# Key and rate products made beside attention instead of in the scan's prep

## The chip, the cores and the metric

The kernel runs on one core of a Trainium2 chip. The core has a matrix engine (TensorE, in the profile PE, its weight loads PEld), a vector engine (VectorE, DVE), an activation engine (ScalarE, ACT), a general engine (GpSimd, POOL) and a queue engine for transfers (SyncE, SP). All work from one on-chip memory; transfers to and from the DRAM run on 16 DMA engines. The metric is the device time of one execution in microseconds (us).

## The reference, cut to what matters

One layer of an encoder: a feed-forward block, a mixing block, a second feed-forward block, for 1024 tokens of width 1024. The mixing block has two groups of 8 heads of 64: attention with three dilated windows, and a recurrent group (RWKV-7) with a forward and a backward scan. What the change touches is the input of the scan:

```python
w_logit = w0 + jnp.einsum('bsdr,drc->bsdc', jnp.tanh(wd), w2)
decay = jnp.exp(-jnp.exp(-jax.nn.softplus(-w_logit) - 0.5))
a = jax.nn.sigmoid(a0 + jnp.einsum('bsdr,drc->bsdc', ad, a2))
kk = (k * k_k).reshape(B, S, H, N)
kk = kk / jnp.maximum(jnp.sqrt(jnp.sum(kk * kk, axis=-1, keepdims=True)), 1e-12)
k_dir = k[:, :, None, :] * (1.0 + (a - 1.0) * k_a)
...
xs = (orient(both(r)), orient(decay), orient(k_dir), orient(both(v)),
      orient(both(kk)), orient(kk[:, :, None, :] * a))
...
    sa = jnp.einsum('dbhvk,dbhk->dbhv', state, kk)
    state = state * w[..., None, :] - sa[..., :, None] * kka[..., None, :] + v[..., :, None] * k[..., None, :]
```

So the scan takes, for each of two directions (`d`), two products that depend on the rate `a`: `kk * a` (here the **rate product**) and `k * (1 + (a - 1) * k_a)` (the **key product**). The second is also used after the scan, for the bonus term.

## The kernel before, in words

The kernel is one program for one core, about 41,000 instructions, all in fp32. `run` (L1167) goes through these stages: first feed-forward; low-rank rates (`low_rank`, L534) and attention's projections; attention; the scan; the finish of the recurrent group; the output projection; the second feed-forward.

**The order of the work.** The program is written against a tile layer: tiles come from pools, a tag in a pool has a number of buffers (`bufs`), and a tile that reuses a buffer waits until all readers and writers of the old tile are done. When the program is built, a planner fixes the order of each engine's queue from the order in the text, priorities and its own estimates of durations; so instructions of neighbouring parts are interleaved. On the chip each queue, SP's and POOL's among them, runs strictly in that order: an instruction that waits holds up all that stand behind it on its engine.

**Streams.** `project_rwkv` (L499) makes one 128-column stream of the recurrent group for all 1024 tokens: it loads columns of `w_in` (tiles `zraw`, halves `zh` and `zl`), multiplies (L510, matmuls `zr`), mixes in the neighbouring tokens (`shift`, L517, its two VectorE steps L524 and L525) and hands the stream, tile `us`, to `stream` (L566). Streams 0 to 3 are r, 4 to 7 are k, 8 to 11 are v. For a k stream, `stream` stores k (L579), normalises it per head (L583 to L599, tile `kr`) and stores that (L600), both by POOL's queue, into the DRAM tensor `rk_d`, in which r, k and kk lie behind one another.

**Attention** (`attention`, L737) goes through 8 heads. In each, `near` (L665) makes scores (L684, L685), subtracts the maximum (VectorE L686), exponentiates (ScalarE L689), transposes (L698, copies L699) and multiplies by the values (L705); the head ends with steps on VectorE (L719 to L729), POOL (L731 to L733) and VectorE (L734). Behind head h one stream is written, in the order 4, 5, 6, 7, 1, 2, 3; in the trace its matmuls lie between those of the heads. Attention's tiles come from the pool `wa` (2 buffers a tag), those of the streams from `zr` (2 buffers a tag where nothing else is said).

**The scan** works in 8 blocks of 128 tokens, each in both directions.
- `prep(n)` (L789) makes for each direction the factors of block n. It loads the summed decays (`th_w`), the rates (`th_a`) and r, k and kk together (`in`, 768 KB in one transfer, one buffer), all for 4 x 128 channels and 128 tokens. Then: exponentials (L811, L812), products with kk and r (L816, L817), the rate product (L820: `(th_a + 1) * kk`, L821: times 0.5 and the inverse decay), the key product (ScalarE L825, four instructions, one for each 128 channels, then VectorE L827), its product with the inverse decay (L828), and a store of the key product (L829, SP's queue, to `kd_d`). Matmuls L836 and VectorE L838 make the small triangular matrices `lm`, transposes L844 and ScalarE L846 the tile `bt`. Part of `lm` goes out to the DRAM (L852).
- `solve(n)` (L856) loads it back in another layout (tile `X`) and inverts on VectorE in 62 small dependent steps (L872, L874) and a transpose (L876).
- `merge(n)` (L879) finishes the inverses with small matmuls (L889, L894, L900).
- `chain(n)` (L918) takes the state through the two 64-token chunks of the block: matmuls L941, L952, L937, copies on ScalarE (L944, L954, L970), the new state on VectorE (L968).

Three sets of block tiles exist, and prep n+3 is written behind chain n (L1300 to L1305). Preps 0 and 1 are written among the four value streams (L1272 to L1275).

**The finish** (`finish_unit`, L975) adds both directions and loads for that, among others, the two key products (`k0`, `k1`, L983).

Of the kernel before, what the change touches and what calls it, by code (L numbers as in the profile page):

```python
# [10 lines left out]
F32 = mybir.dt.float32  # L11
F32R = mybir.dt.float32r
AF = mybir.ActivationFunctionType
OP = mybir.AluOpType
# [4 lines left out]
S, D, DFF, INW = 1024, 1024, 2816, 3456  # L19
# [7 lines left out]
C, NC_, BLK = 64, 16, 2  # L27
TB = C * BLK
# [135 lines left out]
class _Kernel:  # L164
# [333 lines left out]

    def project_rwkv(self, p, psum, x, blocks):  # L499

        nc, V, A, T = self.nc, self.nc.vector, self.nc.scalar, self.nc.tensor
        for c0, n in blocks:
            hl = self.columns(p, ATT + c0 * 128, n * 128)
            for ct in range(c0, c0 + n):
                cs = slice((ct - c0) * 128, (ct - c0 + 1) * 128)
                ps = [psum.tile([128, 512], F32, name="zr", tag="d", bufs=2) for half in range(2)]
                for half in range(2):
                    for k, (h, l) in enumerate(hl):
                        for i, (w, j) in enumerate(((h, 0), (h, 1), (l, 0))):
                            T.matmul(ps[half], w[:, cs], x[half][j][:, k, :], start=(k == 0 and i == 0),  # L510
                                     stop=(k == NK - 1 and i == 2))
# [54 lines left out]
    def stream(self, p, psum, ct, y):  # L566
# [10 lines left out]
        elif ct < 8:  # L577
            i = ct - 4
            self.nc.gpsimd.dma_start(self.rk_d[4 + i], y)  # L579
            sq = p.tile([128, S], F32, name="ksq", tag="u", bufs=1)  # L580
            kr = p.tile([128, S], F32, name="kr", tag="kr", bufs=1)
# [11 lines left out]
            for half in range(2):  # L593
# [195 lines left out]
    def prep(self, n, p, psum, big):  # L789
# [8 lines left out]
        for d in range(2):  # L798
            b = n if d == 0 else NC_ // BLK - 1 - n
            ts = slice(b * TB, (b + 1) * TB)  # L800
            th = {}
            for nm in "wa":
                th[nm] = p.tile([128, 4, TB], F32, name="th_" + nm, tag="th_" + nm, bufs=2)
                self.load(th[nm], self.lr_d[nm][d][:, :, ls].rearrange("a p t -> p a t"))
            x3 = p.tile([128, 3, 4, TB], F32, name="in3", tag="in3", bufs=1)
            self.load(x3.rearrange("p j a t -> p (j a) t"), self.rk_d[:, :, ts].rearrange("a p t -> p a t"))
            x = {nm: x3[:, j, :, ::-1] if d else x3[:, j] for j, nm in enumerate(("r", "k", "kk"))}
            cum = th["w"]
            e1 = self.e1
# [9 lines left out]
            bb = bk[:, :, :, 0:C]  # L819
            V.scalar_tensor_tensor(bb, chunks(th["a"]), 1.0, chunks(x["kk"]), op0=OP.add, op1=OP.mult)  # L820
            V.scalar_tensor_tensor(bb, bb, 0.5, ei, op0=OP.mult, op1=OP.mult)  # L821
            A.copy(bk[64:, :, :, 2 * C:], bk[64:, :, :, 0:C])
            kd = th["a"]
            for pr in range(4):
                A.activation(kd[:, pr, :], kd[:, pr, :], AF.Identity, scale=self.kah[:, pr:pr + 1],  # L825
                             bias=self.ka1[:, pr:pr + 1])
            V.tensor_tensor(kd, kd, x["k"], op=OP.mult)  # L827
            V.tensor_tensor(bk[:, :, :, C:2 * C], chunks(kd), ei, op=OP.mult)  # L828
            self.nc.sync.dma_start(self.kd_d[d][:, :, ls].rearrange("a p t -> p a t"), kd)  # L829
            bt = big.tile([128, BLK, 2, 4, 64], F32, name="bt", tag=f"bt{d}")  # L830
# [144 lines left out]
    def finish_unit(self, p, psum, b, g, x, g2w):  # L975
# [6 lines left out]
        z = {}  # L982
        for nm, src, sl in (("y0", self.y_d[0], ts), ("y1", self.y_d[1], back), ("k0", self.kd_d[0], ts),  # L983
                            ("k1", self.kd_d[1], back), ("r", self.rk_d, ts), ("v", self.v_d, ts)):
            z[nm] = p.tile([128, 2, FB], F32, name="f_" + nm, tag="f_" + nm)
            self.load(z[nm], src[ps2, :, sl].rearrange("a p t -> p a t"))
# [112 lines left out]
    def constants(self):  # L1099
# [67 lines left out]
    def run(self):  # L1167
# [5 lines left out]
        with self.top as top:  # L1173
# [87 lines left out]
            zr, pz = self.pool(s_zr, "zr", 2), self.pool(s_zr, "ps_r", 1, space=PSUM)  # L1261
            streams = [4, 5, 6, 7, 1, 2, 3]
            self.attention(pa, wa, lambda h: self.project_rwkv(zr, pz, x, [(ct, 1) for ct in streams[h:h + 1]]))
            s_at.close()
# [175 lines left out]
```

## Time and profile before

| | |
|---|---|
| median of 3 runs | 2351.09 us (2346.66 to 2355.77) |
| the profiled execution | 2345.14 us |
| its span, first to last instruction | 2343.4 us |
| busy share: PE, DVE, ACT, POOL | 94%, 75%, 44%, 24% |
| attention | about 905 to 1190 us of the span |
| first preps with value streams | about 1190 to 1290 us |
| scan | about 1290 to 1565 us |
| finish | about 1565 to 1640 us |

How to read it: times in the views are microseconds from the start of the span. A row of a group names line, engine, operation, the tile written <- the tiles read, shapes and count, then the busy time of the group in us and the mean of one in ns, then the idle time of the engine ahead of it and what ended it. A row of waits names who waited, for whom, the total in us, how many times, and the longest. A row of the timeline has start, duration, engine, line, operation, tiles, shapes and count, and in brackets the idle time ahead and its end. Durations of neighbouring instructions on one engine overlap a little, so what one costs its queue is the distance between starts. A matmul's busy time is modelled; a busy PE isn't PE at its peak.

### The profile page before, as it was taken

Reading aid. Unit: us, or ns where it says so; the run is one execution under the profiler, and the core shown is the slowest. Engines: PE = TensorE matmul, PEld = TensorE weight load, DVE = VectorE, ACT = ScalarE, POOL = GpSimd, SP = SyncE. Lnnn points to the kernel's source line nnn. Section 1 sums busy time; section 2 is a strip of 40 time slices with the busy share of each in tenths; the row PEclk is TensorE's granted clock in tenths of the full one; section 3 lists DMA queues with packets and bytes.
Section 4 is the critical chain, followed back from the end, with each engine's and each line's share of the span. In section 5 each row is a group of like instructions: output and inputs, shape, how many; then the busy total and the mean of one; then the engine's idle time right before and its main releaser. Section 6 shows DMA issues by size and latency. Waiting matters only on the chain. (4 is left out here: it accounts for less than half of the span.)

```text
span 2343.4 us, 41364 instructions
## 1 busy us (share of the span) xinstructions
PE 2204.7 (94%) x15556; PEld 1783.2 (76%) x15556; DVE 1766.4 (75%) x2870; ACT 1032.5 (44%) x1958; POOL 552.9 (24%) x662
## 2 busy tenths in 40 slices
PE   6999999999999998999996889988799999999997
PEld 4788888878877676788775777765578888887886
DVE  8899999965676244666668878737899999996565
ACT  4333232354567412666545565445442323235453
POOL 6244444410000010111111111122334444441000
PEclk8999999999999999999997899999899999999999
DMA  5344545476661514443268656368434454548555
GB/s 158 99 165 159 173 147 171 161 265 194 196 223 80 219 46 118 119 118 97 64 171 219 170 150 172 106 200 278 153 117 166 167 175 147 173 155 267 192 191 179
DMA packets 357149, 381.97 MB, mean 163 GB/s; under 512 B 73043, under 2 KB 264403, under 8 KB 356949
## 3 DMA queue, kind: packets, MB, share of 16 engines
q1 hardware_dynamic: 309088, 278.53, 39.1%
q0 software_dynamic: 27504, 88.14, 10.0%
q10 hardware_dynamic: 20356, 12.66, 1.8%
q8 instruction: 122, 2.00, 0.4%
q14 instruction: 79, 0.64, 0.1%
HBM read 256.49 MB, written 122.75 MB: 162 GB/s over the span
## 5 line engine op out<-in xcount | busy, mean ns | idle before, releaser
L186 ACT ACTIVATE wh<-raw 128x512 fp32r<-128x512 f32 (+1 forms) x273 | 167.5, 626 | 261.2 <-DVE raw L62 92.2
L187 DVE TENSOR_TENSOR wl<-raw,wh 128x512 fp32r<-128x512 f32 (+1 forms) x273 | 277.3, 1018 | 3.2 <-ACT wh L186 2.3
L81 PE MATMUL gu<-xh,wh 128*128 128x512 f32 x704 | 277.7, 395 | 1.2 <-ACT xh L186 0.8
L81 PE MATMUL gu<-xl,wh 128*128 128x512 f32 x704 | 276.3, 392 | 0.0
L81 PE MATMUL gu<-xh,wl 128*128 128x512 f32 x704 | 275.9, 392 | 0.0
L415 PE MATMUL pd<-gl,gwh 128*128 128x512 f32 x616 | 240.4, 390 | 2.6 <-DVE gl L187 2.6
L415 PE MATMUL pd<-gh,gwh 128*128 128x512 f32 x616 | 239.5, 390 | 0.6 <-DVE row L86 0.6
L415 PE MATMUL pd<-gh,gwl 128*128 128x512 f32 x616 | 239.7, 389 | 0.0
L86 DVE TENSOR_TENSOR row<-gu,row 128x512 f32<-128x512 f32 x308 | 206.7, 683 | 22.1 <-PE gu L81 21.5
L187 DVE TENSOR_TENSOR gwl<-graw,gwh 128x512 fp32r<-128x512 f32 (+1 forms) x176 | 118.0, 674 | 128.6 <-ACT gwh L186 126.5
L116 POOL DMA_DIRECT2D d_hid<-row x154 | 85.1, 553 | 471.8 <-DVE row L114 446.1
L186 ACT ACTIVATE gwh<-graw 128x512 fp32r<-128x512 f32 (+1 forms) x176 | 101.3, 576 | 186.7 <-PE pd L415 152.2
L81 PEld LDWEIGHTS gu<-xh,wh 128*128 128x128 f32 x704 | 133.7, 190 | 30.3 <-ACT xh L186 2.0
L81 PEld LDWEIGHTS gu<-xh,wl 128*128 128x128 f32 x704 | 133.4, 190 | 27.7
L81 PEld LDWEIGHTS gu<-xl,wh 128*128 128x128 f32 x704 | 133.4, 190 | 27.4
L415 PEld LDWEIGHTS pd<-gl,gwh 128*128 128x128 f32 x616 | 115.7, 188 | 28.1 <-DVE gl L187 4.4
L415 PEld LDWEIGHTS pd<-gh,gwh 128*128 128x128 f32 x616 | 115.6, 188 | 25.3 <-DVE row L86 1.0
L415 PEld LDWEIGHTS pd<-gh,gwl 128*128 128x128 f32 x616 | 115.7, 188 | 23.9
L94 ACT ACTIVATE row<-row 128x512 f32<-128x512 f32 x44 | 27.9, 633 | 227.1 <-DVE row L86 219.6
L187 DVE TENSOR_TENSOR gl<-raw,gh 128x512 fp32r<-128x512 f32 x160 | 112.2, 713 | 15.6 <-ACT gh L186 15.1
L145 POOL TENSOR_TENSOR ws<-ws 128x512 f32<-128x512 f32 x88 | 114.4, 1300 | 1.2
L186 ACT ACTIVATE gh<-raw 128x512 fp32r<-128x512 f32 x160 | 98.1, 621 | 36.4 <-DMA raw<-in_ffn_w_down_dram 21.7
(354 smaller groups left out, 5258.8 us busy)
## 6 DMA issues: line engine op xcount, KB each, us to landing
d_hid<-row POOLq DMA_DIRECT2D x154, 256.0 KB, 2.4
graw<-d_hid SPq DMA_DIRECT2D x132, 256.0 KB, 2.9
raw<-in_ffn_w_gate_dram SPq DMA_DIRECT2D x88, 256.0 KB, 3.1
raw<-in_ffn_w_up_dram SPq DMA_DIRECT2D x88, 256.0 KB, 3.3
ws<-in_ffn_w_down_dram SPq DMA_DIRECT2D x88, 256.0 KB, 4.4
d_ws<-ws POOLq DMA_DIRECT2D x88, 256.0 KB, 2.3
raw<-d_ws SPq DMA_DIRECT2D x88, 256.0 KB, 2.7
raw<-in_ffn_w_down_dram SPq DMA_DIRECT2D x66, 256.0 KB, 3.5
```

The source lines that it names most:

```text
L81: self.K.nc.tensor.matmul(ps, a[:, k, :], b[:, k, :], start=(k == 0 and i == 0), stop=(k == 3 and i == 2))
L86: add = lambda o, x: V.tensor_tensor(o, ps, x, op=OP.add)
L94: A.activation(y[:, 0], y[:, 0], AF.Silu)
L116: put = lambda n, y: G.dma_start(self.hid[n - 1, j // 2], y)
L145: G.tensor_tensor(o, a, b, op=OP.subtract)
L186: self.nc.scalar.activation(h, src, AF.Copy)
L187: (eng or self.nc.vector).tensor_tensor(l, src, h, op=OP.subtract)
L415: T.matmul(ps[x], a[:, ts], b, start=(m == 0 and k == 0), stop=(m == NM - 1 and k == 2))
```

## The change

Both products are made once, for all 1024 tokens, when a key stream is made beside attention. For each key stream and direction a tile `ra` of 128x1024 rates is loaded by SP's queue from `lr_d` (512 KB), ahead of the stream's columns, into a tag of its own in attention's pool (two buffers, so 8 KB more of each partition). In `stream`, behind the normalised key, ScalarE and VectorE make the key product in two halves of 512 tokens (tiles `rb`, in the tag `vts`, two buffers, which only the value streams used), VectorE makes the rate product in one instruction of 1024 tokens in place, and POOL's queue stores them: two stores of 256 KB and one of 512 KB. The backward direction reads k and kk in reverse. The plain k is no longer stored.

`prep` loads four things instead of three: decays, the rate product (`ka`, two buffers), the key product (`kd`, one buffer), and r and kk (`in2`, 512 KB, one buffer). The instructions L820, L825 and L827 and the store L829 go; the one that was L821 now reads `ka` and L828 reads `kd`. The finish reads the key products from the new tensors `ak_d`.

```diff
-    def project_rwkv(self, p, psum, x, blocks):
+    def project_rwkv(self, p, psum, x, blocks, wide=None):
         for c0, n in blocks:
+            for d in range(2) if 4 <= c0 < 8 else ():
+                a = wide.tile([128, S], F32, name="ra", tag="ra")
+                self.load(a, self.lr_d["a"][d][c0 - 4])
+                self.rates.append(a)
             hl = self.columns(p, ATT + c0 * 128, n * 128)
...
         elif ct < 8:
             i = ct - 4
-            self.nc.gpsimd.dma_start(self.rk_d[4 + i], y)
...
-            self.nc.gpsimd.dma_start(self.rk_d[8 + i], kr)
+            self.nc.gpsimd.dma_start(self.rk_d[4 + i], kr)
+            for d in range(2):
+                a = self.rates.pop(0)
+                turned = lambda z: z[:, ::-1] if d else z
+                for half in range(2):
+                    sl = slice(half * 512, half * 512 + 512)
+                    b = p.tile([128, 512], F32, name="rb", tag="vts")
+                    A.activation(b, a[:, sl], AF.Identity, scale=self.kah[:, i:i + 1], bias=self.ka1[:, i:i + 1])
+                    V.tensor_tensor(b, b, turned(y)[:, sl], op=OP.mult)
+                    self.nc.gpsimd.dma_start(self.ak_d[d][4 + i][:, sl], b)
+                V.scalar_tensor_tensor(a, a, 1.0, turned(kr), op0=OP.add, op1=OP.mult)
+                self.nc.gpsimd.dma_start(self.ak_d[d][i], a)
...
-            th = {}
-            for nm in "wa":
-                th[nm] = p.tile([128, 4, TB], F32, name="th_" + nm, tag="th_" + nm, bufs=2)
-                self.load(th[nm], self.lr_d[nm][d][:, :, ls].rearrange("a p t -> p a t"))
-            x3 = p.tile([128, 3, 4, TB], F32, name="in3", tag="in3", bufs=1)
+            cum = p.tile([128, 4, TB], F32, name="th_w", tag="th_w", bufs=2)
+            self.load(cum, self.lr_d["w"][d][:, :, ls].rearrange("a p t -> p a t"))
+            ak = [p.tile([128, 4, TB], F32, name=nm, tag=nm, bufs=b) for nm, b in (("ka", 2), ("kd", 1))]
+            for j in range(2):
+                self.load(ak[j], self.ak_d[d][4 * j:4 * j + 4, :, ls].rearrange("a p t -> p a t"))
+            x3 = p.tile([128, 2, 4, TB], F32, name="in2", tag="in2", bufs=1)
             self.load(x3.rearrange("p j a t -> p (j a) t"), self.rk_d[:, :, ts].rearrange("a p t -> p a t"))
...
-            V.scalar_tensor_tensor(bb, chunks(th["a"]), 1.0, chunks(x["kk"]), op0=OP.add, op1=OP.mult)
-            V.scalar_tensor_tensor(bb, bb, 0.5, ei, op0=OP.mult, op1=OP.mult)
+            V.scalar_tensor_tensor(bb, chunks(ak[0]), 0.5, ei, op0=OP.mult, op1=OP.mult)
             A.copy(bk[64:, :, :, 2 * C:], bk[64:, :, :, 0:C])
-            kd = th["a"]
-            for pr in range(4):
-                A.activation(kd[:, pr, :], kd[:, pr, :], AF.Identity, scale=self.kah[:, pr:pr + 1],
-                             bias=self.ka1[:, pr:pr + 1])
-            V.tensor_tensor(kd, kd, x["k"], op=OP.mult)
-            V.tensor_tensor(bk[:, :, :, C:2 * C], chunks(kd), ei, op=OP.mult)
-            self.nc.sync.dma_start(self.kd_d[d][:, :, ls].rearrange("a p t -> p a t"), kd)
+            V.tensor_tensor(bk[:, :, :, C:2 * C], chunks(ak[1]), ei, op=OP.mult)
...
-        self.rk_d, self.v_d = self.dram("rk", [12, 128, S]), self.dram("v", [4, 128, S])
+        self.rk_d, self.v_d = self.dram("rk", [8, 128, S]), self.dram("v", [4, 128, S])
...
-        self.kd_d = [self.dram(f"kd{d}", [4, 128, S]) for d in range(2)]
+        self.ak_d = [self.dram(f"ak{d}", [8, 128, S]) for d in range(2)]
```

More of the change, by code (lines that the diff above doesn't have):

```diff
@@ L982, in finish_unit @@
         z = {}
-        for nm, src, sl in (("y0", self.y_d[0], ts), ("y1", self.y_d[1], back), ("k0", self.kd_d[0], ts),
-                            ("k1", self.kd_d[1], back), ("r", self.rk_d, ts), ("v", self.v_d, ts)):
+        for nm, src, sl in (("y0", self.y_d[0], ts), ("y1", self.y_d[1], back), ("k0", self.ak_d[0][4:], ts),
+                            ("k1", self.ak_d[1][4:], back), ("r", self.rk_d, ts), ("v", self.v_d, ts)):
             z[nm] = p.tile([128, 2, FB], F32, name="f_" + nm, tag="f_" + nm)
@@ L1261, in run @@
             zr, pz = self.pool(s_zr, "zr", 2), self.pool(s_zr, "ps_r", 1, space=PSUM)
-            streams = [4, 5, 6, 7, 1, 2, 3]
-            self.attention(pa, wa, lambda h: self.project_rwkv(zr, pz, x, [(ct, 1) for ct in streams[h:h + 1]]))
+            streams, self.rates = [4, 5, 6, 7, 1, 2, 3], []
+            self.attention(pa, wa, lambda h: self.project_rwkv(zr, pz, x, [(ct, 1) for ct in streams[h:h + 1]], wa))
             s_at.close()
```

3 lines of the change are left out of this document (1 added, 2 removed).

## The prediction

> **What bounds the kernel now.** I read the views in this order: the page's head, the busy time of each engine in windows cut at the stage borders, the engines' waits inside the two stages that the change touches, and VectorE in order of time.
>
> ```profile
> span 2343.4 us, 41364 instructions
> PE 2204.7 (94%) x15556; PEld 1783.2 (76%) x15556; DVE 1766.4 (75%) x2870; ACT 1032.5 (44%) x1958; POOL 552.9 (24%) x662
> ```
>
> By the page TensorE bounds everything. The windows below split that average; their columns are the span of the window, the busy time (and instructions) of PE, PEld, DVE, ACT and POOL, then the granted clock, the DMA share and GB/s. The first is attention, the second the first preps with the value streams, the third the scan up to the last full solve.
>
> ```profile
> 905.00:1190.00 285.00, 276.34 (x2665) 222.98 (x2664) 168.79 (x453) 163.96 (x384) 37.58 (x55) 0.98 0.39 107
> 1190.00:1290.00 100.00, 77.48 (x768) 63.07 (x768) 79.86 (x204) 56.80 (x110) 11.17 (x19) 0.83 0.80 211
> 1290.00:1500.00 210.00, 188.20 (x3621) 157.43 (x3622) 165.71 (x480) 113.24 (x214) 28.27 (x53) 0.91 0.57 155
> ```
>
> In attention PE is busy 276.3 of 285 us: it sets the pace, and VectorE (169) and ScalarE (164) have over 110 us to spare each. From 1190 to 1500 PE leaves 310 - 265.7 = 44.3 us idle, and its clock is 0.83 and 0.91. VectorE in order of time shows what it waits for: the end of one block's solve (L876) and the first product of the next (L872).
>
> ```profile
> 1257.47 1.05 DVE L876 STREAM_TRANSPOSE X<-Ti 128x512 f32<-128x512 f32 x1
> 1258.44 0.15 DVE L872 TENSOR_TENSOR ttmp<-X,Ti 128x31 f32<-128x31 f32 x1
> ...
> 1339.65 1.06 DVE L876 STREAM_TRANSPOSE X<-Ti 128x512 f32<-128x512 f32 x1
> 1341.27 0.19 DVE L872 TENSOR_TENSOR ttmp<-X,Ti 128x31 f32<-128x31 f32 x1 [0.56 <-DMA X<-d_x]
> ...
> 1498.18 1.06 DVE L876 STREAM_TRANSPOSE X<-Ti 128x512 f32<-128x512 f32 x1
> 1501.32 0.19 DVE L872 TENSOR_TENSOR ttmp<-X,Ti 128x31 f32<-128x31 f32 x1 [0.86 <-DMA X<-d_x]
> ```
>
> One solve follows another with a gap of 1 to 3 us, and merge and chain of a block can only start behind its solve. Seven solves end from 1257.5 to 1498.2, six steps of 40 us. In those 40 us VectorE's one queue also holds the prep of a later block, two directions of it. So from 1190 to 1500 VectorE's queue, its work plus its waits, is the path. The waits in 1190 to 1500:
>
> ```profile
> DVE ttmp L872 <- DMA X<-d_x: 10.4, 4, 5.8
> DVE sv L968 <- PE st L937: 9.3, 6, 3.8
> DVE lm L838 <- PE lp L836: 9.0, 11, 2.0
> DVE pr L816 <- DMA in<-d_rk: 6.6, 5, 2.0
> DVE th_a L827 <- ACT th_a L825: 6.5, 5, 2.0
> ```
>
> **What the scan loses (removed).** One direction of a prep, on VectorE:
>
> ```profile
> 1214.17 0.68 DVE L816 TENSOR_TENSOR pr<-in,e 128x512 f32<-128x512 f32 x1
> 1214.77 0.69 DVE L817 TENSOR_TENSOR pr<-in,e 128x512 f32<-128x512 f32 x1
> 1215.38 0.68 DVE L820 SCALAR_TENSOR_TENSOR bk<-th_a,in 128x512 f32<-128x512 f32 x1
> 1215.98 0.28 DVE L187 TENSOR_TENSOR zl<-zraw,zh 128x128 fp32r<-128x128 f32 x1
> 1216.18 0.68 DVE L821 SCALAR_TENSOR_TENSOR bk<-bk,th_w 128x512 f32<-128x512 f32 x1
> 1218.56 0.69 DVE L827 TENSOR_TENSOR th_a<-th_a,in 128x512 f32<-128x512 f32 x1 [1.69 <-ACT th_a L825]
> 1219.28 0.69 DVE L828 TENSOR_TENSOR bk<-th_a,th_w 128x512 f32<-128x512 f32 x1
> ```
>
> L820 and L827 go; L821 and L828 stay with other operands. Each is shown with 0.68 us, but starts are 0.60 us apart (1214.17, 1214.77, 1215.38), so one costs its queue 0.60. There are 16 of each:
>
> ```profile
> L820 DVE SCALAR_TENSOR_TENSOR bk<-th_a,in 128x512 f32<-128x512 f32 x16 | 11.0, 688 | 1.6 <-DMA in<-d_rk 1.4
> L827 DVE TENSOR_TENSOR th_a<-th_a,in 128x512 f32<-128x512 f32 x16 | 11.0, 688 | 6.6 <-ACT th_a L825 6.5
> L825 ACT ACTIVATE th_a<-th_a,ka,kah 128x128 f32<-128x128 f32 x64 | 28.3, 486 | 5.3 <-DVE bk L820 5.1
> ```
>
> 32 x 0.60 = 19.2 us leave VectorE, all inside 1190 to 1500. Not all reaches the end: PE is itself 86% busy there, and where VectorE comes earlier it meets a later PE or DMA (the 10.4, 9.3 and 9.0 above). The bounds are 0 and -19.2; I take two thirds, -13, because the waits listed are the minority of VectorE's 310 us.
>
> The 64 ACTIVATEs of L825 (28.3 us) leave ScalarE, which is busy 170 of 310 us; by themselves nothing. But they stand between L820 and L827, and VectorE waits 6.5 us for them. Also, the tile "in" has one buffer, and L827 is its last reader, 4.4 us behind L816; afterwards L817, 0.6 us behind, is the last reader, so that part of the 6.6 us waits for the next load goes. Bounds 0 and -13.1. What is late next is the tile "kd", one buffer too: its load waits for the L828 of the direction before, on SP's queue, with the load of r and kk written behind it; both wait for less than the old load did, as L828 now follows without ScalarE. I take half of the 6.5, -3.
>
> **Transfers and queues of the scan.** Median landing times, KB each:
>
> ```profile
> in<-d_rk SPq DMA_DIRECT2D x16, 768.0 KB, 5.9
> th_a<-d_a SPq DMA_DIRECT2D x16, 256.0 KB, 5.7
> d_kd<-th_a SPq DMA_DIRECT2D x16, 256.0 KB, 2.8
> ```
>
> Per direction SP issued three loads and a store, and will issue four loads: no change in SP's issue time. Bytes fall from 256+256+768+256 = 1536 to 1280 KB. A third of "in" becomes the tile kd; a 256 KB load lands after 5.7 us and a 768 KB one after 5.9, so the loads are no faster. The store waited for L827 with later loads behind it; that block goes. I count 0, inside the bounds above. The final stage reads the key product from the new tensors, written long before: nothing on the path, 0.
>
> **What attention gains (added).** Four key streams, two directions each: 8 STTs of 128x1024 and 16 products of 128x512 on VectorE, 16 ACTIVATEs of 128x512 on ScalarE, 24 new stores and 4 dropped on POOL's queue, 8 loads on SP's. The nearest rows in 905 to 1640:
>
> ```profile
> L524 DVE SCALAR_TENSOR_TENSOR us<-u,c_rwkv_mu_prev,us 128x1023 f32<-128x1023 f32 x12 | 15.4, 1280 | 11.9 <-ACT us L523 11.8
> L523 ACT ACTIVATE us<-zr,mu 128x512 f32<-128x512 f32 x22 | 15.1, 686 | 0.8 <-POOL ya L732 0.8
> L579 POOL DMA_DIRECT2D d_rk<-us x4 | 2.3, 584 | 21.2 <-ACT sb L631 5.3 <-DVE us L525 5.3 <-issue 5.3
> ```
>
> VectorE: 8 x 1.28 + 16 x 0.60 = 19.8 us. ScalarE: 16 x 0.69 = 11.0. POOL: 20 x 0.58 = 11.7, on an engine that is busy 37.6 of 285. The work does not shrink, it moves: VectorE gets back what it gave, at a place where it is not the pace. VectorE goes from 59 to 66% busy there, ScalarE from 58 to 61%. The cover is PE's 276 us. If all of it were gone the cost would be 19.8 for VectorE or more by a wait (below). PE's own waits in attention say how thin the cover is:
>
> ```profile
> PE zr L510 <- ACT zh L186: 2.6, 1, 2.6
> PE pt L637 <- ACT sb L631: 2.3, 1, 2.3
> PE s L626 <- DMA qp<-d_q: 1.7, 1, 1.7
> PE s L684 <- DVE nm L686: 1.0, 4, 0.3
> ```
>
> These are 7.6 us, of which 5.9 on ScalarE and VectorE. I take half as much again, +3. The new rate tiles make the attention pool 8 KB larger; its first loads wait for older tiles at that place. PE's one wait on such a load is the 1.7 above: it could go or double, so bounds of -1.7 and +1.7; I take 0. SP's 8 loads of 512 KB run early, at a DMA share of 0.39: 0.
>
> **The sum** against the profiled execution (2345.14 us, the span of 2343.4 and 1.7 around it): -13 - 3 + 3 = -13. That execution lies 6 us under the median of the runs (2351.09); the difference carries over: **2338**.
>
> **A rule weighed against this.** PE's clock is 0.98 in attention, and 0.83 and 0.91 in the scan, where it has the long waits. The Trainium skill, "TensorE: Matmul & The Clock Gate", section "What's actually happening", says that an idle window of about 3.4 us halves TensorE's clock, and a busy one restores it. By that rule each stall the change puts into attention costs again in slow matmuls, and each one it takes from the scan pays twice. The windows agree as to the direction.
>
> **The rivals.**
> *The others take over.* VectorE's 16 us become waits for PE, the X round trip and the loads: L872, L968 and L838 already wait 28.7 us. For: PE is 90% busy from 1290 to 1500. Against: the solves stand back to back. Only -3 + 3, and perhaps a little, remains: 2349 (2345 to 2357).
>
> *The clock comes along* (this is what the rule above would give). PE is busy 265.7 us from 1190 to 1500 at a mean clock near 0.88; at 0.94 the same work is done in 249, 17 us less, on top of the 13: 2321. For: the fall to 0.83 lies where VectorE holds PE. Against: part of those waits (DMA, "issue") stays.
>
> *Slower: the product tile waits for its own store.* The four key products of a stream go through the tag "vts", which has two buffers. The third ACTIVATE must wait until the first product is stored: 0.69 on VectorE and 3.1 to landing, 3.8 us, with ScalarE's queue, the exponentials of L689 among it, standing behind it, and PE behind those. The store is on POOL's queue, where L731 waits for the end of a head:
>
> ```profile
> POOL far L731 <- DVE cc L727: 106.1, 8, 18.5
> d_rk<-us POOLq DMA_DIRECT2D x8, 512.0 KB, 3.1
> ```
>
> Behind half of a mean such wait (106.1 / 8 / 2 = 6.6) the stall is 10.4 us a stream, 42 for four; less the 16 saved that is +26: **2377** (2357 to 2385). It decides from (16 + 12) / 4 = 7 us a stream. For: queues are in order. Against: the order of each queue is planned with such waits in view, and ScalarE can hold other work between the products.
>
> *It does not do what it says*: if the products are issued behind attention, prep 0 waits for them. The streams concerned are the first four, 100 us ahead of 1190: I give it nothing of its own.
>
> **How the numbers follow.** 0.5% of 2351 is 12 us, about what a measurement of this kernel can tell from no change: faster means under 2339, slower over 2363. Forecast (2338, own range 2326 to 2345): 0.42, of which 0.30 under 2339. Others take over: 0.18, all within. Clock: 0.15, faster. Slower rival: 0.25, of which 0.21 over 2363 and 0.04 within. Faster 0.30 + 0.15 = 0.45; same 0.12 + 0.18 + 0.04 = 0.34; slower 0.21. The range 2318 to 2374 leaves out about 0.05 below and 0.13 above.
>
> **What would show it.** Right: the solves end less than 38 us apart, VectorE's wait on L825 is gone, PE's idle time from the first prep on falls by ten or more, attention stays within 5 us of 285, its PE clock at 0.98. Wrong: ScalarE's new ACTIVATE waiting for a DMA store, PE's waits on L689's tile growing (slower rival); waits of VectorE for PE or X growing by as much as its work fell (others take over); or a different planned order that moves stalls to other places than those named.

## The result and the profile after

The changed kernel takes **2335.79 us** (median of 8 runs, 2327.99 to 2341.98) against 2347.59 of the kernel before (8 runs beside it, 2341.89 to 2355.77): ratio **0.9947**, 95% interval 0.9928 to 0.9967. That is 12 us, by the ratio 0.53%, faster; the forecast was 13.

The page's head and the three windows of the prediction, after the change:

```profile
span 2332.0 us, 41360 instructions
PE 2205.8 (95%) x15556; PEld 1784.2 (77%) x15556; DVE 1763.1 (76%) x2862; ACT 1016.8 (44%) x1910; POOL 565.2 (24%) x682
```

```profile
905.00:1190.00 285.00, 272.15 (x2613) 217.60 (x2612) 181.60 (x467) 170.07 (x390) 49.86 (x66) 0.96 0.48 139
1190.00:1290.00 100.00, 88.00 (x916) 72.37 (x915) 79.22 (x214) 49.67 (x94) 14.69 (x32) 0.85 0.81 212
1290.00:1500.00 210.00, 194.00 (x3799) 162.50 (x3799) 155.82 (x461) 102.96 (x185) 27.72 (x52) 0.92 0.52 147
```

Work moved as planned: VectorE has 12.8 us more in the first window (181.6 against 168.8) and 10.5 us less in the other two. But the windows stand still while the stages moved, so read the stages by their own borders. Three marks serve: the last step of the first head and of the last head, and the last store of the scan's result. Before, then after, in the timeline:

```profile
963.15 0.69 DVE L734 TENSOR_REDUCE ss_a<-far 128x8 f32<-128x512 f32 x1 [2.23 <-POOL far L733]
...
1179.78 0.69 DVE L734 TENSOR_REDUCE ss_a<-far 128x8 f32<-128x512 f32 x1 [2.48 <-POOL e L1155]
...
1564.70 1.43 ACTq L972 DMA_DIRECT2D d_y<-yb  x2
```

```profile
965.11 0.69 DVE L748 TENSOR_REDUCE ss_a<-far 128x8 f32<-128x512 f32 x1 [2.75 <-POOL far L747]
...
1190.68 0.69 DVE L748 TENSOR_REDUCE ss_a<-far 128x8 f32<-128x512 f32 x1 [2.48 <-POOL e L1162]
...
1559.00 0.92 ACTq L979 DMA_DIRECT2D d_y<-yb  x2
```

The span fell by 11.4 us: first head +2.0, attention (from mark to mark) 216.6 to 225.6, **+8.9**; scan 384.9 to 368.3, **-16.6**; the rest (finish and second feed-forward) 778.7 to 773.0, -5.7. So half of what the two profiles differ by lies behind the scan. That part can't be laid to the products: over all kernels of this study it is anywhere from 771.5 to 779.2, with either scan ahead of it (table below). Each kernel has one profile, so whether it belongs to a kernel's planned order or to the one execution stays open.

**In the scan** the gain stands at its head. The first product of the first two directions, the first step of the first solve, and the ends of solves (the first one before is in the prediction), before and after:

```profile
1190.60 0.69 DVE L816 TENSOR_TENSOR pr<-in,e 128x512 f32<-128x512 f32 x1 [2.05 <-DMA in<-d_rk]
1202.10 0.68 DVE L816 TENSOR_TENSOR pr<-in,e 128x512 f32<-128x512 f32 x1
...
1224.93 0.18 DVE L872 TENSOR_TENSOR ttmp<-X,Ti 128x31 f32<-128x31 f32 x1
...
1526.30 1.06 DVE L876 STREAM_TRANSPOSE X<-Ti 128x512 f32<-128x512 f32 x1
```

```profile
1200.07 0.69 DVE L830 TENSOR_TENSOR pr<-in,e 128x512 f32<-128x512 f32 x1
1207.10 0.69 DVE L830 TENSOR_TENSOR pr<-in,e 128x512 f32<-128x512 f32 x1 [0.67 <-DMA in<-d_rk]
...
1226.23 0.18 DVE L879 TENSOR_TENSOR ttmp<-X,Ti 128x31 f32<-128x31 f32 x1
...
1251.36 1.08 DVE L883 STREAM_TRANSPOSE X<-Ti 128x512 f32<-128x512 f32 x1
...
1487.82 1.08 DVE L883 STREAM_TRANSPOSE X<-Ti 128x512 f32<-128x512 f32 x1
...
1517.12 1.04 DVE L883 STREAM_TRANSPOSE X<-Ti 128x512 f32<-128x512 f32 x1
```

One direction followed the other after 11.5 us, now after 7.0. The first solve (its end is the transpose, L876 before, L883 after) ended 77.7 us behind attention (1257.47 - 1179.78) and now ends 60.7 behind it: 17 us of lead. Of these, 9.6 are an earlier start (35.6 behind attention instead of 45.2), and 7.4 a shorter solve (25.1 instead of 32.5): its steps are the same, but by their durations some 10 us of other instructions stand between them in VectorE's queue, instead of 19. From the first solve to the eighth it then takes 265.8 us instead of 268.8: the pace itself hardly changed. What VectorE waits for from 1190 to 1500, after:

```profile
DVE pr L830 <- PE y L944: 11.9, 3, 6.0
DVE sv L975 <- PE st L944: 10.4, 4, 6.8
DVE bk L834 <- ACT th_w L826: 8.0, 5, 5.8
DVE ttmp L879 <- DMA X<-d_x: 7.2, 3, 3.2
```

The wait for L825 (6.5) is gone. In its place stand a wait for the exponential of the decays (L826, 8.0) and one for PE at the start of later preps (11.9).

**In attention** PE does the same matmuls in more time. The window from mark to mark, before and after:

```profile
963.15:1179.78 216.63, 214.94 (x2180) 174.32 (x2179) 135.46 (x373) 132.82 (x310) 29.96 (x38) 1.00 0.32 90
```

```profile
965.11:1190.68 225.57, 222.46 (x2181) 178.02 (x2180) 152.80 (x399) 142.76 (x326) 44.92 (x58) 0.99 0.43 129
```

2180 and 2181 matmuls, 214.9 and 222.5 us "busy": for the same work, busy time itself grew by 7.5 us, and PE's idle time only from 1.7 to 3.1. A part is the clock. Before, it was 1.00 in all of this stretch; after, it fell once:

```profile
1044.00:1056.00 12.00, 12.00 (x78) 10.03 (x77) 7.37 (x22) 9.21 (x17) 2.17 (x5) 0.86 0.28 94
```

That is an estimated 12 x 0.14 = 1.7 us. With this and the 1.4 us of idle time taken off, some 6 of the 8.9 us stand in PE's busy time, without a wait that the rows name. So the 97% busy of the prediction was no measure of how PE was held up. The Trainium skill, "Trainium Kernel Development and Optimization", section "Performance Expectations", calls matmul busy time a bad metric for how close a kernel is to roofline, and the weight loads' busy share a good one. This case agrees as to the first: PE is 99% busy in both windows; the weight loads are busy for 80 and 79% of them.

### The profile page after: what moved, and what is told of

It reads as the page before. It is cut to its first block, busy times and chain, and to the rows that moved or that the text cites. A ratio compares the mean times of both kernels' runs of the same rounds, so it can differ in the third digit from the quotient of the medians.

```text
span 2332.0 us, 41360 instructions
## 1 busy us (share of the span) xinstructions
PE 2205.8 (95%) x15556; PEld 1784.2 (77%) x15556; DVE 1763.1 (76%) x2862; ACT 1016.8 (44%) x1910; POOL 565.2 (24%) x682
## 5 line engine op out<-in xcount | busy, mean ns | idle before, releaser
L81 PEld LDWEIGHTS gu<-xh,wl 128*128 128x128 f32 x704 | 133.0, 189 | 27.5
```

The lines of the kernel that those rows point to most:

```text
L81: self.K.nc.tensor.matmul(ps, a[:, k, :], b[:, k, :], start=(k == 0 and i == 0), stop=(k == 3 and i == 2))
```

## The experiments

All kernels in one table; the three stage times are of each one's profiled execution, by the same marks. "Scan" names which scan's instructions the kernel has. Each ratio is to runs of the kernel before on the same chip in turn (its medians there 2343.9 to 2347.7; beside the single runs 2344.70, and 2334.66 beside 11), so medians of different rows compare to a few us only.

| kernel | scan | attention | scan us | rest | time, median | ratio (95%) |
|---|---|---|---|---|---|---|
| before | old | 216.6 | 384.9 | 778.7 | 2347.59 | 1 |
| after | new | 225.6 | 368.3 | 773.0 | 2335.79 | 0.9947 (0.9928-0.9967) |
| 1 products only | old | 225.5 | 385.7 | 778.7 | 2353.48 | 1.0027 (1.0010-1.0044) |
| 2 scan only | new | 216.4 | 372.0 | 779.2 | 2326.52 | 0.9909 (0.9894-0.9924) |
| 3 VectorE work back | new, more VectorE | 223.3 | 382.7 | 774.1 | 2347.79 | 1.0009 (0.9984-1.0033) |
| 4 ScalarE work back | new, more ScalarE | 225.1 | 380.4 | 771.5 | 2343.06 | 0.9986 (0.9970-1.0002) |
| 5 transfers only | new | 224.0 | 366.8 | 771.8 | 2331.85, one run | |
| 6 no ACTIVATEs | new | 220.3 | 373.7 | 775.1 | 2335.36, one run | |
| 7 ACTIVATEs only | new | 223.7 | 369.8 | 772.2 | 2332.85, one run | |
| 8 k apart | old | 217.1 | 389.5 | 772.6 | 2343.54, one run | |
| 9 rates placed first | new | 225.3 | 365.1 | 776.0 | 2334.26 | 0.9952 (0.9934-0.9970) |
| 10 also loaded late | new | 221.6 | 368.0 | 773.0 | 2333.85 | 0.9950 (0.9934-0.9967) |
| 11 no loads | new | 224.7 | 375.2 | 772.3 | 2342.60, one run | |
| 12 no stores | new | 218.7 | 368.7 | 774.9 | 2332.56 | 0.9949 (0.9927-0.9972) |

Two readings rest on many kernels: all nine kernels with the new scan alone have 365 to 375 us there (mean 370), the three with the old one 385 to 390 (mean 387), **-17**; and attention takes 216.4 to 217.1 us where nothing is added, 218.7 to 225.6 where something is. Experiments 1, 3, 4 and 9 have the changed kernel's instructions in attention and show 223.3 to 225.5, so a difference of 2 us between two single profiles can't be read.

### 1 and 2: the two halves of the change

Experiment 1 is the kernel before with the change's loads, products and stores beside attention, and `prep` left as it was. Experiment 2 is the changed kernel without them: the products are left out, and the new scan loads the plain rates and keys in their place.

```diff
# 1, in before
+            for d in range(2) if 4 <= c0 < 8 else ():
+                a = wide.tile([128, S], F32, name="ra", tag="ra")
...
+                V.scalar_tensor_tensor(a, a, 1.0, turned(kr), op0=OP.add, op1=OP.mult)
+                self.nc.gpsimd.dma_start(self.ak_d[d][i], a)
# 2, in after
-            for d in range(2) if 4 <= c0 < 8 else ():
...
-                self.nc.gpsimd.dma_start(self.ak_d[d][i], a)
-                self.load(ak[j], self.ak_d[d][4 * j:4 * j + 4, :, ls].rearrange("a p t -> p a t"))
+                self.load(ak[j], (self.lr_d["a"][d], self.k_d)[j][:, :, ls].rearrange("a p t -> p a t"))
```

> The products are made and stored beside attention as in the changed kernel, but prep works as before and doesn't read them. Theory (VectorE's queue paces preps and scan, attention pays a little): attention's end stays about 11 us late, as in the profile after (1190 against 1179), the scan keeps its old length, so 8 to 12 us over the kernel before: 2356 to 2360. Rival (what attention shows is only another order of the same work and is given back by 1260): within 4 us of before.

> Prep works as after, with loads of the same sizes and shapes, but of the plain rates and the plain key; nothing is made beside attention, so the two products are left out of the computation. Theory: the scan's gain without attention's cost, 20 to 24 us under the kernel before: 2324 to 2328. Rival (the scan gains because the products come early or in another order, not because VectorE has less to do): no more than the 12 us of the whole change.

Measured: the products alone cost 5.8 us by medians against 2347.72, by the ratio 0.27% = 6.3 us. The scan alone gains 21.2 (0.91% = 21.4). So 1 lies between its theory (8 to 12) and its rival (within 4), and 2 is what its theory said (20 to 24). The sum is -15, the whole change -12, which the intervals allow. Attention is 225.5 us in 1 and 216.4 in 2, as in after and before:

```profile
960.21:1176.57 216.36, 214.79 (x2180) 174.18 (x2179) 135.46 (x372) 132.83 (x310) 29.82 (x38) 1.00 0.32 90
```

So the gain is the scan's and the loss attention's, and each is larger than the prediction had it: -21 for -16, and +6 to +9 for +3. In the profiles the scan's stage is less clearly above the forecast: it is 13.0 us shorter in 2 than before, 16.6 in the changed kernel, 17 in the mean over all kernels.

### 3 and 4: what in the scan is worth what

Experiment 3 gives VectorE 32 instructions back, experiment 4 gives ScalarE 64 small copies back. Both repeat an instruction that is there.

```diff
# 3
-            V.scalar_tensor_tensor(bb, chunks(ak[0]), 0.5, ei, op0=OP.mult, op1=OP.mult)
+            for _ in range(3):
+                V.scalar_tensor_tensor(bb, chunks(ak[0]), 0.5, ei, op0=OP.mult, op1=OP.mult)
# 4
             A.copy(bk[64:, :, :, 2 * C:], bk[64:, :, :, 0:C])
+            for pr in range(4):
+                A.copy(bk[64:, pr, :, 2 * C:], bk[64:, pr, :, 0:C])
```

> The changed kernel with VectorE's remaining product of the rate and the inverse decay issued three times over instead of once: the 32 instructions of 128x512 that the change took from VectorE's queue in the preps are back, and nothing else. Theory: 32 x 0.60 = 19 us come back nearly whole, plus 15 to 19 over the changed kernel: 2351 to 2355. Rival (others take over, PE or the loads): at most plus 6.

> The changed kernel with four more copies of 64x128 on ScalarE in each direction of a prep, behind the copy of the rate product, 64 in all as many as the instructions that left ScalarE there. Theory (ScalarE isn't the pace, only its place between two VectorE steps was): plus 0 to 4 over the changed kernel. Rival (the gain of the scan is ScalarE's 28 us): plus 8 or more.

VectorE's 32 instructions cost 12.0 us over the changed kernel by medians, 14.6 by the ratios (1.0009 - 0.9947). That is under the 15 to 19 expected and over the rival's 6 (with the intervals of both ratios, 7 to 22): about two thirds of 19.2, and that share was the forecast's own. ScalarE's copies cost 7.3 by medians, 9.2 by the ratios (3 to 15), where the theory said 0 to 4 and the rival 8 or more. They are 14.3 us of work, half of the 28.3 that the change took from ScalarE, on an engine that is idle for about half of the scan:

```profile
L837 ACT COPY bk<-bk 64x128 f32<-64x128 f32 x64 | 14.3, 291 | 0.5
```

What VectorE waits for from 1200 to 1520, with the copies (first fence), in the changed kernel (second), and in experiment 3 (third):

```profile
DVE sv L977 <- PE st L946: 19.9, 5, 8.3
DVE wol L1064 <- ACT woh L1063: 12.5, 5, 6.4
...
DVE pr L830 <- PE y L946: 2.8, 1, 2.8
```

```profile
DVE pr L830 <- PE y L944: 11.9, 3, 6.0
DVE sv L975 <- PE st L944: 10.4, 4, 6.8
...
DVE wol L1062 <- ACT woh L1061: 3.0, 3, 2.0
```

```profile
DVE wol L1063 <- ACT woh L1062: 14.3, 6, 8.4
```

With the copies, VectorE waits 19 us longer for the chain's state (L977) and for the output weights, which ScalarE makes. But its wait for PE at the start of later preps is 9 us shorter, and the wait for the output weights is as long in experiment 3, which has no copy more. So the rows don't show by which wait the copies cost their 7 to 9 us; that it goes by the copies of the chain, which stand in ScalarE's queue behind them and on which PE waits, is argued. What is shown is that a low share of busy time didn't make the work free.

Nor is giving work back the reverse of taking it away. The first solve starts 36.4 and 34.5 us behind attention in 3 and 4 (35.6 in the changed kernel, 45.2 before) and ends 64.3 and 62.2 behind it: of the 17 us won there, 3.6 and 1.5 are given back. The rest is paid later: the first to the eighth solve take 274.1 and 277.5 us instead of 265.8. Both experiments put instructions back, but not the way from VectorE over ScalarE to VectorE that the key product took before. So 12 to 15 and 7 to 9 are together of the size of the 21 of experiment 2, but they are no breakdown of it.

### 8: the earlier release of the tile alone

The kernel before, with k in a tile of its own; all products stay in `prep`.

```diff
-            x3 = p.tile([128, 3, 4, TB], F32, name="in3", tag="in3", bufs=1)
+            x3 = p.tile([128, 2, 4, TB], F32, name="in2", tag="in2", bufs=1)
...
+            xk = p.tile([128, 4, TB], F32, name="ink", tag="ink", bufs=1)
+            self.load(xk, self.k_d[:, :, ts].rearrange("a p t -> p a t"))
...
```

> The kernel before with k loaded into a tile of its own, so that the tile of r and kk is free behind its own last reader and not behind the key product; all products stay in the scan. First theory: the scan's gain at its head (first solve's end 77.7 us behind attention before, 60.7 after) comes for the larger part from that release: 64 to 70 us here, and the time 5 to 10 under the kernel before. Rival: it comes from the instructions that are gone, release alone gives little: 75 to 79 us, time within 4 of before.

The time, one run, is 1.2 us under the kernel before beside it, as the rival said; the end of the first solve lies between the two expectations. It comes 72.7 us behind attention (1252.28 - 1179.62), 5 of the 17 us earlier, and all of that by an earlier start (39.7 behind attention instead of 45.2). But the eighth solve ends 274.5 later, and the scan lasts 389.5, no less than before.

```profile
1252.28 1.07 DVE L879 STREAM_TRANSPOSE X<-Ti 128x512 f32<-128x512 f32 x1
...
1526.77 1.06 DVE L879 STREAM_TRANSPOSE X<-Ti 128x512 f32<-128x512 f32 x1
```

An earlier release helps the first preps and is given back later. That this is so because VectorE's and ScalarE's queues are as long as they were is argued, not shown.

### 5, 6, 7, 11 and 12: which part costs attention its nine us

Each leaves one kind of work out of the changed kernel's attention: 5 all 40 compute instructions, 6 the ACTIVATEs, 7 VectorE's products, 11 the loads, 12 the stores.

```diff
# 5: in place of the products
+                    self.nc.gpsimd.dma_start(self.ak_d[d][4 + i][:, sl], y[:, sl])
+                self.nc.gpsimd.dma_start(self.ak_d[d][i], a)
# 6
-                    A.activation(b, a[:, sl], AF.Identity, scale=self.kah[:, i:i + 1], bias=self.ka1[:, i:i + 1])
-                    V.tensor_tensor(b, b, turned(y)[:, sl], op=OP.mult)
+                    V.tensor_tensor(b, a[:, sl], turned(y)[:, sl], op=OP.mult)
# 7
-                    V.tensor_tensor(b, b, turned(y)[:, sl], op=OP.mult)
-                V.scalar_tensor_tensor(a, a, 1.0, turned(kr), op0=OP.add, op1=OP.mult)
# 11
-                self.load(a, self.lr_d["a"][d][c0 - 4])
-                    A.activation(b, a[:, sl], AF.Identity, scale=self.kah[:, i:i + 1], bias=self.ka1[:, i:i + 1])
+                    A.activation(b, y[:, sl], AF.Identity, scale=self.kah[:, i:i + 1], bias=self.ka1[:, i:i + 1])
-                V.scalar_tensor_tensor(a, a, 1.0, turned(kr), op0=OP.add, op1=OP.mult)
+                V.scalar_tensor_tensor(a, y, 1.0, turned(kr), op0=OP.add, op1=OP.mult)
# 12
+            self.nc.gpsimd.dma_start(self.k_d[i], y)
-                    self.nc.gpsimd.dma_start(self.ak_d[d][4 + i][:, sl], b)
-                self.nc.gpsimd.dma_start(self.ak_d[d][i], a)
-                self.load(ak[j], self.ak_d[d][4 * j:4 * j + 4, :, ls].rearrange("a p t -> p a t"))
+                self.load(ak[j], (self.lr_d["a"][d], self.k_d)[j][:, :, ls].rearrange("a p t -> p a t"))
...
```

> The changed kernel with the 16 ACTIVATEs and 24 products of attention left out; the rates are still loaded ahead, and the key stream and the rates are stored in the products' place, so the same transfers, queues and tiles remain (the products are missing from the output). Attention from its first to its last head's end was 216.6 us before and 225.6 after. Theory (the nine us are paid by the products' instructions, which disturb TensorE's short gaps): 217 to 219 us, end of the first solve 60 to 62 us behind attention, time 2325 to 2329. Rival (the nine us come from the transfers, the queues' order and the larger pool): 224 to 226 us, time 2333 to 2338.

> The changed kernel without the 16 ACTIVATEs in attention: the key product is rate times key, its affine step left out; VectorE's 24 products, loads and stores stay. Attention 225.6 us after, 216.6 before. If VectorE's products carry the cost: 223 to 226 us. If the ACTIVATEs in ScalarE's queue, between the exponentials, carry it: 217 to 219. If each has its share by busy time (11 of 31 us): about 222.

> The changed kernel without VectorE's 24 products in attention (they are left out); the 16 ACTIVATEs, loads and stores stay. Counterpart of the run before: if VectorE's products carry the cost, attention is 217 to 219 us; if the ACTIVATEs do, 223 to 226; if each by its share, about 220.

> The changed kernel with the eight loads of rates in attention left out: the products take the key stream in the rates' place (so the output lacks the rates), all other instructions, tiles and stores stay. Attention was 216.6 us before, 225.6 with the change, 224.0 with loads and stores but no products, 221.6 with the loads behind the columns. Theory (the loads of rates ahead of the stream's columns on SP's queue carry most of the nine us): 216.5 to 220 us. Rival (it is the planned order and the stores, whatever is added; the loads are hidden): 222 to 226 us.

> The changed kernel with the 24 stores of products in attention left out and the plain key stored as before; the rates are loaded and all products made beside attention, but the scan loads the plain rates and keys in their place, with the same instructions (so the output lacks the products). Attention was 216.6 us before, 225.6 with the change, 224.0 with loads and stores alone, 224.7 without the loads. Theory (the stores are what those two kernels share: 24 entries more in POOL's queue, between the steps that end a head): 217 to 220 us, and the time 2326 to 2330, as without any products. Rival (no single part: whatever is added, the order planned for the queues of attention is another one and a few us worse): 221 to 226 us, time 2331 to 2337.

The windows of attention of 5, 6 and 12, in that order:

```profile
967.49:1191.53 224.04, 219.25 (x2178) 177.29 (x2178) 137.97 (x378) 133.53 (x315) 39.60 (x54) 0.98 0.40 116
```

```profile
964.55:1184.83 220.28, 219.48 (x2181) 176.15 (x2180) 153.25 (x400) 134.05 (x312) 40.57 (x58) 1.00 0.44 132
```

```profile
962.85:1181.57 218.72, 218.25 (x2181) 177.33 (x2181) 155.96 (x400) 142.90 (x326) 32.20 (x38) 0.99 0.37 104
```

The theory of experiment 5, that the products' instructions carry the cost, fell: VectorE's busy time is up by 2.5 us over before and ScalarE's by 0.7, instead of 17.3 and 9.9, and attention still takes 224.0. 6 and 7 by themselves would point at the ACTIVATEs: 220.3 without them, and 223.7 with them alone, which is what was expected if they carry the cost. But 5 leaves them out too, so the parts don't add up. The loads don't carry it either (224.7 without them). Without the stores it is **218.7**, with all 40 instructions and all loads in place and the four stores of the plain key back: of 8.9 us, 6.9 less in that profile.

The time does not confirm this. The ratio of 12 is 0.9949, that of the changed kernel 0.9947: half a us apart, give or take 7 by the two intervals. That of experiment 2, with the same scan and nothing added to attention, is 0.9909. So without the stores the kernel is still 3 to 16 us slower than without all that was added. The time expected (2326 to 2330) was missed; 2332.56 lies in the rival's range.

Can 24 stores of some 0.55 us each on POOL's queue delay others? ScalarE's waits for POOL in attention (who, for whom, total, times, longest), before, after, and the largest in 6:

```profile
ACT us L523 <- POOL ya L732: 0.8, 1, 0.8
```

```profile
ACT ksq L586 <- POOL ya L746: 1.8, 1, 1.8
ACT sb L703 <- POOL ya L746: 1.4, 1, 1.4
...
ACT us L527 <- POOL ya L746: 0.8, 1, 0.8
```

```profile
ACT u L526 <- POOL ya L745: 4.5, 1, 4.5
```

They are 0.8 us before and 4.0 after; with the stores left out the views show none. But 6 has 5.5 us of them in all, and its attention is 5 us shorter than the changed kernel's: the one doesn't go with the other. Nor do the stores make them. Ahead of the first step that POOL does at the end of a head, POOL stands idle in each of the seven heads, and what it waits for is VectorE (changed kernel):

```profile
POOL far L745 <- DVE cc L741: 89.7, 7, 19.1
```

One such end of a head in the timeline of the changed kernel:

```profile
1071.40 1.04 POOL L745 TENSOR_TENSOR far<-far,cc 128x512 f32<-128x512 f32 x1 [13.18 <-DVE cc L741]
...
1072.89 0.68 DVE L743 TENSOR_TENSOR ya<-po,cc 128x512 f32<-128x512 f32 x1
...
1073.49 1.28 DVE L529 SCALAR_TENSOR_TENSOR us<-u,c_rwkv_mu_next,us 128x1023 f32<-128x1023 f32 x1
...
1073.72 2.10 POOL L746 TENSOR_TENSOR ya<-ya,far 128x512 f32<-128x512 f32 x1 [1.27 <-issue]
...
1075.85 0.37 ACTq L749 DMA_DIRECT2D d_ya<-ya  x1
...
1076.32 1.15 ACT L586 ACTIVATE ksq<-us,c_rwkv_k_k 128x1024 f32<-128x1024 f32 x1 [1.77 <-POOL ya L746]
```

No store of a product lies among POOL's three steps or just ahead of them; L746 starts when VectorE has made `ya` (L743). The head's result is stored by **ScalarE's** queue (L749), which stands there until POOL's L746 is done, and ScalarE's work behind it waits. So the rows show how ScalarE comes to wait for POOL, but not that the stores cause it, nor that PE pays for it.

Which of the added parts costs attention its nine us stays open. The stores are the one whose absence shows most in a profile. But the planner makes another order for the whole of attention in each of these kernels, and the rival of experiment 12, that no single part carries the cost, is not refuted.

### 9 and 10: where the rates lie and when they are loaded

```diff
# 9
+            self.ra = [wa.tile([128, S], F32, name="ra", tag="ra") for d in range(2)]
             self.bias12 = wa.tile([128, 640], F32, name="k_bias12", bufs=1)
...
-                a = wide.tile([128, S], F32, name="ra", tag="ra")
+                a = self.ra.pop(0) if self.ra else wide.tile([128, S], F32, name="ra", tag="ra")
# 10: as 9, and
+            hl = self.columns(p, ATT + c0 * 128, n * 128)
             for d in range(2) if 4 <= c0 < 8 else ():
...
-            hl = self.columns(p, ATT + c0 * 128, n * 128)
```

> The changed kernel, with the two rate tiles taken first from attention's pool: they get the 8 KB that are new, and every other tile of attention lies where it lay before the change. In the changed kernel the first load of attention waits 95 us for an older tile at its new place and is issued at 909.5 us, 12.6 us later than before (896.9); attention starts about 2.5 us later and its first head, 39.9 us, is 5 longer than before. Theory (the larger pool's late first loads cause that part): first load near 897 again, PE's wait for qp back under 2 us, first head's end 2 to 3 us earlier, attention 219 to 223 us instead of 225.6, time 3 to 7 us under the changed kernel, 2329 to 2333. Rival (the place of the tiles is hidden; the planned order of the products and their instructions cost the nine us): attention 224.5 to 226.5, time within 3 of the changed kernel.

> As the run before, and the rates of a stream are loaded behind the stream's eight column loads on SP's queue, not ahead of them. Theory (two loads of 512 KB ahead of the columns delay the stream's matmuls, which stand in PE's queue between those of the heads): attention 1 to 4 us shorter than in the run before, time 1 to 4 us less. Rival (the columns come early enough either way): attention within 1 us, time within 2 us of the run before.

The tiles' place does what was said of it and is worth nothing. The first load, that of `k_bias`, is issued at 898.5 in 9 and at 909.5 in the changed kernel. That is eleven us earlier again, yet the first head ends at 966.0 (965.1 in the changed kernel) and attention takes 225.3: the rival held. Loading late takes attention to 221.6, 3.7 less, as the theory said, but the median, 2333.85, is that of 9 (2334.26). Both are as fast as the changed kernel within their intervals; no kernel here that makes the products is shown to beat it.

## Why the prediction was right, and where it was not

The time, 2335.8 against 2338, and its sign are right, and so is the sum, -12 for -13. But it came out right in part by luck. By the two halves on the chip the scan gained more than was forecast (-21 for -16) and attention cost more (+6 to +9 for +3), and the two cancelled. By the stages of the two profiles the scan's -16.6 is the forecast's -16, attention with its first head is +10.9, and what makes up for it is -5.7 behind the scan, for which the prediction had no term.

- **-13 for VectorE's 32 instructions: the size is borne out, the place is not.** Giving them back costs 12 to 15 us. But only 3.6 of that lie ahead of the first solve's end, where the change won 17. (The list of VectorE's waits beside this term leaves out one of 6.8 us, `yat` L1072 for its load; the sum doesn't use it.)
- **-3 for the waits in `prep`: mis-sized.** "By themselves nothing", the step said of ScalarE's ACTIVATEs, as ScalarE is busy for only 170 of 310 us. Experiment 4 put half of that time back, at another place, and paid 7 to 9 us. And the first solve starts 9.6 us earlier, which neither VectorE's instructions nor ScalarE's copies take back when they are put in again (36.4 and 34.5 us behind attention): so at the head of the scan the waits, or the order that the planner makes without them, were worth more than -3. The tile that comes free earlier has 5.5 of these 9.6 (experiment 8, where it is worth nothing at the end); what the way over ScalarE is worth has no run of its own.
- **+3 for attention: mis-sized, +6 to +9.** The cover named, PE's 276 busy us, was no cover: the +3 was taken from PE's listed waits, but between the marks PE's idle time grew by only 1.4 us, and its busy time by 7.5 for the same matmuls. Which of the added parts does it stays open.
- **0 for attention's pool: right.** PE's wait for qp rose from 1.7 to 5.0, but moving the tiles back (experiment 9) gave nothing.
- **Solves "less than 38 us apart": wrong.** 17 us are won by the end of the first solve; then the steps of a solve are (1487.82 - 1251.36) / 6 = 39.4 us instead of 40.1. There the rival *others take over* describes what happens: waits for PE take the place of work. Still, the instructions matter there too: with experiment 3's, the first to the eighth solve took 274.1 instead of 265.8.
- **The other signs.** The wait on L825 is gone, and PE's idle time from the first prep's first product to the scan's last store fell from 374.1 - 323.8 = 50.3 to 358.9 - 323.3 = 35.6 us: right. The windows, before and after:

```profile
1190.56:1564.70 374.14, 323.84 (x5877) 268.75 (x5875) 272.03 (x761) 198.19 (x378) 54.42 (x93) 0.90 0.62 168
```

```profile
1200.10:1559.00 358.90, 323.30 (x5887) 269.88 (x5886) 253.75 (x729) 173.03 (x316) 55.65 (x94) 0.90 0.60 165
```

  Attention within 5 us (it is +8.9) and its clock at 0.98 (it is 0.96 in that window): wrong.
- ***The clock comes along*: no.** The clock rose from 0.83 to 0.85 and from 0.91 to 0.92 while PE idled 15 us less. The rule of the Trainium skill that was weighed ("TensorE: Matmul & The Clock Gate", section "What's actually happening") has the direction right and, here, a small size, in attention too: one fall of the clock, an estimated 1.7 us.
- ***Slower, by the product tile's wait for its store*: no.** ScalarE never waits for a store of `rb` in the changed kernel. The wait exists where the order is another: 5.1 us in experiment 11, 1.4 in 7. That the queue that was feared, POOL's, costs time is not shown.

## What to carry to other kernels

Before work is moved "beside" an engine that looks full, or onto one that looks idle, don't take a share of busy time for an answer: here PE's 97% hid nine us that attention lost, and 14 us of copies on a half idle ScalarE cost 7 to 9. Split a change into its two halves on the chip; the whole (-12) hid +6 and -21, and only the halves showed that the scan's own gain is well above the total. Be slower with smaller parts: work that is put back is not paid where it was won, and parts that are left out one by one need not add up when the planner makes another order each time. And ask what stands behind a store in its queue: one that waits for another engine's result makes the work behind it wait (1.77 us in the timeline above). Before such a wait is called the cost, look at what released the engine waited for, and whether the kernels that have the wait are the slow ones.

## What the runs showed of the hardware

POOL's steps at the end of a head run longer beside certain VectorE work. In groups, before and after:

```profile
L732 POOL TENSOR_TENSOR ya<-ya,far 128x512 f32<-128x512 f32 x7 | 8.6, 1228 | 1.5 <-POOL far L731 1.0
```

```profile
L746 POOL TENSOR_TENSOR ya<-ya,far 128x512 f32<-128x512 f32 x7 | 10.2, 1461 | 4.2 <-POOL far L745 2.7 <-issue 1.3
```

Single ones of the three steps (L745 to L747) take 1.0 to 1.3 us or more, up to 2.1, and in every kernel of the study that has any of 1.9 and over, these lie over a wide VectorE instruction with two inputs from on-chip memory: in the timeline above L746 takes 2.10 under L529, 1.28 long. Another pair:

```profile
999.59 1.22 DVE L676 TENSOR_TENSOR sq<-qp,sq 64x1024 fp32r<-64x1024 f32 x1
...
999.65 2.08 POOL L745 TENSOR_TENSOR far<-far,cc 128x512 f32<-128x512 f32 x1 [13.56 <-DVE cc L741]
```

L745 takes 1.04 where what runs beside it is VectorE's product with a matmul's result and subtractions of 128 columns. The Trainium skill, "SBUF — State Buffer", section "Who interferes with whom", says this: such a VectorE instruction and a GpSimd one that reads the memory share a port and exclude each other. The rows agree, about 1 us for each meeting. It also lengthened ScalarE's wait in the timeline above, as L746 takes 1.2 to 1.3 where nothing wide lies over it. What these meetings cost attention is not shown: the three steps take 27.5 us in the seven heads after and 23.3 before, and without the stores, where attention was 6.9 us shorter, 25.7.
